# A third pair of convolution projections by seven quarter products instead of two full chunks, with its weight sums in DRAM

## The chip, the cores and the metric

The kernel runs on one core of a Trainium2 chip. The metric is the device time of one execution in microseconds (us), the median of three runs. Besides, one execution was taken with the hardware profiler; its trace gives each engine's instructions, waits and transfers. The engines are PE (matrix products; PEld is its weight load), DVE (vector), ACT (scalar engine), POOL (GpSimd, which here mostly issues transfers) and SP (which issues the weight loads).

## The reference

One block of an encoder in float32, 512 tokens by 1024 features: a short gated convolution and a four-head retention side by side, merged by gates, then a feed-forward part.

```python
h = rmsnorm(x, g_mix)
proj = h @ w_in
xc, gb, gc, q, k, v, g_sw, gate_a, gate_r = split(proj)   # xc, gb, gc: 1024 columns each
u = gc * xc
conv = sum(u_pad[:, tap:tap + s] * w_conv[tap] for tap in range(3))
y_a = (gb * conv) @ w_a_out
ret = group_norm(retention_fwd(q, k, v) + retention_bwd(q, k, v))   # 4 heads
y_r = (ret * silu(g_sw)) @ w_r_out
x = x + (sigmoid(gate_a) * y_a + sigmoid(gate_r) * y_r) @ w_o
h2 = rmsnorm(x, g_ffn)
x = x + (silu(h2 @ w_ff_gate) * (h2 @ w_ff_up)) @ w_ff_down
return rmsnorm(x, g_final)
```

The change is about `xc` and `gc` (called x and C here), about a quarter of their columns: 512 to 767.

## The kernel before

**Products.** Float32 is kept by splitting each operand into a rounded part (hi) and the rest (lo). A product of two such pairs takes three matmuls, hi by hi, hi by lo and lo by hi (`mm3`, lines 337 to 341). For a weight tile (128 x 1024) this means: the raw tile is loaded by SP into the pool `raw` (10 buffers), ACT casts it to hi (line 200), DVE subtracts to get lo (line 201), both in the pool `wpool` (5 pairs).

**Two ways to do a projection.** A *chunk* is 256 columns of `w_in`: two loads of 512 KB, and `feature_major` (line 347) with 2 x 8 x 3 = 48 matmuls of 512 token columns (lines 339 to 341). A *quad* does two chunks at once by a scheme of seven products in place of eight (`fm_quad`, line 383): the weights of both are cut into quarters, sums of quarters are formed (t1 to t4), and each of the forms b11, t1, t2, b21, t3, t4, b22 is multiplied by a form of the activations. Each such product (`prod`, line 372) has 2 x 4 x 3 = 24 matmuls of 256 columns (line 380). The first product is copied out of its PSUM bank by ACT (`snap`, line 429, its copy at line 431) before the third product (t2) is added in the same bank; further copies stand behind t2 and t3.

**Sums of weights.** For most quads the sums t1 to t4 are formed by DVE on the raw tiles (line 298). For the quads listed in `SUMMED` they are formed in DRAM ahead of time: POOL issues a copy (line 271) and an accumulating transfer (line 269) for each sum, one step of the list at a time, behind stores of the v and gate projections (`sum_step`, line 262). Before the change these are the first two quads of the feed-forward part.

**Order of the work.** After a start-up and the q and k of three heads come six quads of v, swish gate and branch gates in a token-major form (line 424, up to 323.6 us), then `mix_quads` (line 821): a quad each for x and C of parts 0 and 1 of the convolution (a part is 256 columns), and one for B of both. Behind each quad of x and C stands the convolution (`conv`), behind the third quad `z_forms` (line 782): ACT and DVE split the results into hi and lo, and POOL stores them to DRAM (`z<-t`, line 626); they are read back for the product with `w_a_out` much later. Then `load_head(0)` loads q (hi, lo: `qh`, `ql`), a table, v and the gate of the first head; `do_scores` forms its scores (24 matmuls), `split_v` splits v, `do_mix(2)` does part 2 of the convolution by three chunks x, C and B, and the loop over the heads begins with `do_pv`; part 3 follows inside the loop by three chunks.

The plan is a list of weight units in the order of use; weights are loaded `LEAD` = 4 units ahead of the one that is prepared and prepared (cast, subtract) `AHEAD` = 2 units ahead of their use. A scheduler places the instructions of all engines in their final order, so that independent work (scores, chunks, quads) may be mixed on PE. Small tiles of 128 x 512 for copies and for hi and lo of the stores come from one pool of 9 buffers (`t512`); a buffer that a store reads is free when the store has landed.

Of the kernel before, what the change touches and what calls it, by code (L numbers as in the profile page):

```python
# [1 line left out]

# [1 line left out]

# [65 lines left out]
    return (q, "b21"), (q + 1, "b11") if q + 1 < NQ else None  # L70


def plan():

    out = []  # L80

    def a(name, col):
        out.append(("c", name, 0, 8, col, 256))

    def b(name, row, nk, col, nc):
        out.append(("c", name, row, nk, col, nc))

    def quad(c0, c1):
        for name in FORMS:
            for u in (0, 2):  # L90
                out.append(("q", ("w", c0, c1), name, u, 2))

    for h in range(EARLY):
        for r in (0, 512):
            b("w_in", r, 4, (C_Q + h * QK, C_K + h * QK), 512)
    for h in range(HEADS):
        quad(C_V + h * VD, C_G + h * VD)
        if h >= EARLY:
            a("w_in", C_Q + h * QK)
            a("w_in", C_K + h * QK)  # L100
    for c in (0, 512):
        quad(C_GA + c, C_GR + c)
    for c0, c1 in ((C_XC, C_GC), (C_XC + 256, C_GC + 256), (C_GB, C_GB + 256)):
        for name in FORMS:
            out.append(("q", ("x", c0, c1), name, 0, 4))
    for s in (2, 3):
        for c in (C_XC, C_GC, C_GB):
            a("w_in", c + s * 256)
    for h in range(HEADS):
        for c in (0, 512):  # L110
            b("w_r_out", h * VD, 4, c, 512)
    for name in FORMS:
        for u in (0, 2):
            out.append(("q", ("a",), name, u, 2))
    for r in (0, 512):
        for c in (0, 512):
            b("w_o", r, 4, c, 512)
    def f(q, *names):
        for n in names:
            out.append(("q", ("f", q), n, 0, 4))  # L120

    for q, name in FIRST_PRODUCTS:
        f(q, name)
    for q0, n in FF_PARTS:
        for q in range(q0, q0 + n):
            between, behind = beside(q)
            f(q, "t1", "t2")
            if between:
                f(*between)
            f(q, "t3")  # L130
            if behind:
                f(*behind)
            f(q, "t4", "b22")
        units = [(name, u) for name in FORMS for u in range(0, n, 2)]
# [13 lines left out]

SUMMED = (("f", 0), ("f", 1))


def loads():
# [17 lines left out]
def block_kernel(ctx: ExitStack, tc: tile.TileContext, xw0, xw, xT, xtok, wpack, wquad, cols, decs, rot, g_ffn, g_final, out):  # L172
# [15 lines left out]
    def bigtile(dt=F32, n=4):  # L188
        return big.tile([P, n, 512], dt, tag="big", name="big", padded_shape=[P, 4, 512])
# [28 lines left out]
    pos = [0]  # L218
    block = [0]

    made = []
    ready = []

# [8 lines left out]
    def prefetch_block(loads, splits, inbig):  # L232
        i = block[0]
        block[0] += 1
        st = [rawtile(), rawtile()]
        units = []
        for c in range(2):
            if loads:
                loads(c)
            nc.sync.dma_start(st[c], wpack[i][:, c * QH:(c + 1) * QH])  # L240
        for c in range(2):
            hi, lo = unit(inbig)
            units.append((hi, lo))
            split(st[c], hi, lo)
            if splits:
                splits(c)
        return units
# [6 lines left out]
    def quarter(quad, name, u=0):  # L254
        return wquad[next(i for i, x in enumerate(QUARTERS) if x[1:4] == (quad, name, u))]

    steps = [(quad, f, g, add) for group in (
        (("t1", "b11", 0), ("t3", "b22", 0)), (("t1", "b12", 1), ("t3", "b12", 1)),
        (("t2", "t1", 0),), (("t2", "b22", 1),), (("t4", "t2", 0),), (("t4", "b21", 1),))
        for quad in SUMMED for f, g, add in group]  # L260

    def sum_step(behind=None):

# [165 lines left out]
    def snap(ps):  # L429
        t = t512()  # L430
        nc.scalar.copy(t, ps)  # L431
        return t
# [305 lines left out]
    def do_quad(left, right, func, func_left=None):  # L738
        def ev_sum(dst, o, f):
            def ev(tt, t):  # L740
                if f:
                    nc.scalar.activation(t, t, f)
                last = store(dst[:, o + tt, :], t)
                if tt and not o:
                    sum_step(last)
            return ev

        def ev21(tt, ps):
            t = t512()
            nc.scalar.activation(t, ps, func_left or AF.Copy)  # L750
            last = store(left[:, 2 + tt, :], t)
            if tt:
                turn_one()
                sum_step(last)
        strassen(4, xforms, ev_sum(left, 0, func_left), ev21, ev_sum(right, 2, func), ev_sum(right, 0, func))
# [12 lines left out]
    def conv(m, b, u, c):  # L768

        nc.scalar.activation(c, u[:, 0:512], AF.Copy, scale=wconv[:, 3 * b:3 * b + 1])  # L770
        for tap in (1, 2):
            nc.vector.scalar_tensor_tensor(
                out=c, in0=u[:, tap:tap + 512], scalar=wconv[:, 3 * b + tap:3 * b + tap + 1],
                in1=c, op0=ALU.mult, op1=ALU.add)

    def u_tile():
        u = misctile(2 * 514, "u").rearrange("p (m n) -> p m n", m=2)
        nc.vector.memset(u[:, :, 0:1], 0.0)
        nc.vector.memset(u[:, :, 513:514], 0.0)
        return u  # L780

    def z_forms(s, z):

        x1, x2 = z[:, :, 0:256], z[:, :, 256:512]

        def put(j, t):
            n = t.shape[1]
            hl = [t512(F32R)[:, 0:256 * n].rearrange("p (f t) -> p f t", f=n) for _ in range(2)]
            split(t, *hl)
            for d, x in zip(zd[j], hl):  # L790
                store(d[:, :, s, :], x.bitcast(F32))
# [9 lines left out]
    def do_mix(s):  # L801
        us, c = [], bigtile()[:, 0:2, :]
        feature_major(xg, lambda m, ps: us.append(snap(ps)))
        u = u_tile()

        def ev_c(m, ps):
            nc.vector.tensor_tensor(out=u[:, m, 1:513], in0=ps, in1=us[m], op=ALU.mult)
            conv(m, 2 * s + m, u[:, m], c[:, m])
        feature_major(xg, ev_c)

        def ev_b(m, ps):
            nc.vector.tensor_tensor(out=c[:, m], in0=ps, in1=c[:, m], op=ALU.mult)
        feature_major(xg, ev_b)
        z_forms(s, c)

    T1, T2 = slice(0, 256), slice(256, 512)

    def halves(t):
        return t.rearrange("p (m t) -> p m t", m=2)

    def mix_quads():

        c = bigtile().rearrange("p (s m) t -> p s m t", s=2)
        for s in range(2):
            u, got = u_tile(), {}

            def ev21(ps):
                nc.vector.tensor_tensor(out=u[:, :, 257:513], in0=halves(ps), in1=halves(got["c2"]), op=ALU.mult)

            def ev12(t):  # L830
                nc.vector.tensor_tensor(out=u[:, :, 1:257], in0=halves(got["x1"]), in1=halves(t), op=ALU.mult)
            fm_quad(xf, lambda t: got.update(x1=t), ev21, lambda t: got.update(c2=t), ev12)
            for m in range(2):
                conv(m, 2 * s + m, u[:, m], c[:, s, m])

        def times(s, t):
            def ev(b):
                o = c[:, s, :, t]
                nc.vector.tensor_tensor(out=o, in0=halves(b), in1=o, op=ALU.mult)
            return ev  # L840
        fm_quad(xf, times(0, T1), times(0, T2), times(1, T2), times(1, T1))
        for s in range(2):
            z_forms(s, c[:, s])


    def load(src, dt=F32):
        t = bigtile(dt)
        nc.sync.dma_start(t if dt == F32 else t.bitcast(F32), src)
        return t

    def load_head(h):
# [76 lines left out]
                    nc.vector.tensor_tensor(out=t, in0=t, in1=sgr[half][:, nb, :], op=ALU.mult)  # L928
            token_major(yr, 0, 1, ev)

    mix_quads()
    nxt = load_head(0)
    p = do_scores(nxt[0], nxt[1])
    vv, sg = split_v(nxt[2]), nxt[3]
    do_mix(2)
# [419 lines left out]
```

## Time and profile before

| what | value |
|---|---|
| time of the runs, median (lowest to highest) | 1027.11 us (1026.5 to 1027.32) |
| the profiled execution | 1027.93 us, its span 1026.1 us |
| granted PE clock | 0.999 |
| PE busy | 1018.1 us of the span |
| LDWEIGHTS (PEld) busy | 887.9 us |
| DVE busy / ACT busy / POOL busy | 886.3 / 535.5 / 125.0 us |
| moved by DMA | 187.66 MB |

A row of a group in the profile has the line, engine, operation, the tiles (out<-in), the shape and the count, then the busy time and the mean of one in ns, then the idle time of the engine ahead of them and what ended it. A row of the timeline or the chain has the start in us and the duration. Matmuls are pipelined, and their ends are modelled: how many follow each other in a stretch tells more than the duration of one. In the order of the program the numbers behind a tile's name tell its buffers apart; a row has a line, an operation and its tiles, and `waits` names semaphores, those of DMAs (DMAHW for SP's, DMASW for POOL's) among them.

### The profile page before, as it was taken

What the parts mean: (1) busy time and instruction counts of PE and PEld (TensorE: products, weight loads), DVE (VectorE), ACT (ScalarE), POOL (GpSimd) and SP (SyncE); (2) the same over time, 40 slices, a digit from 0 to 9 for tenths busy, and PEclk for the clock granted to TensorE, in tenths of its full rate; (3) what the DMA queues carried; (4) which work ended last, traced back from release to release, by engine and by line L of the source; (5) the groups of instructions that cost most, each with busy time, mean ns of one, the idle gap of its engine ahead of it and who ended that gap; (6) DMA issues with size and microseconds to landing.
All of it is one profiled execution on the core that took longest, in us unless ns stands there. A gap on an engine that the chain in (4) does not pass through costs nothing.

```text
span 1026.1 us, 14780 instructions
## 1 busy us (share of the span) xinstructions
PE 1018.1 (99%) x5610; PEld 887.9 (87%) x5610; DVE 886.3 (86%) x1151; ACT 535.5 (52%) x728; POOL 125.0 (12%) x205
## 2 busy tenths in 40 slices
PE   9999999999999999999999999999999999999997
PEld 7888888888888998888888888889998999899986
DVE  7878998969798988797999998569998999889996
ACT  7547655553656455342542334356654565556554
POOL 0030231222212003202011000000002000110011
PEclk9999999999999999999999999999999999999999
DMA  9525597794767657828177525633318522663513
GB/s 346 195 83 183 172 299 211 213 312 153 255 203 238 254 200 256 323 81 314 52 277 285 208 94 176 236 102 121 122 44 220 177 87 83 193 156 103 164 29 96
DMA packets 51304, 187.66 MB, mean 183 GB/s; under 512 B 6880, under 2 KB 7008, under 8 KB 47264
## 3 DMA queue, kind: packets, MB, share of 16 engines
q1 hardware_dynamic: 36448, 133.19, 37.5%
q0 software_dynamic: 14496, 53.23, 17.5%
q8 instruction: 44, 0.72, 0.3%
q10 hardware_dynamic: 288, 0.29, 0.1%
q14 instruction: 28, 0.23, 0.1%
HBM read 148.14 MB, written 46.92 MB: 190 GB/s over the span
## 4 chain that ended last, share of the span: by engine, by line
PE 97%; DVE 1%; DMA 1%; issue 0%; POOL 0%; ACT 0%; POOLq 0%; DVEq 0%; ACTq 0%
PE bank L424 34%; PE bank L380 28%; PE bank L339 11%; PE bank L341 11%; PE bank L340 11%; DMA raw<-wquad 1%; PE bank L470 0%; PE bank L1030 0%; PE bank L981 0%; PE bank L655 0%; DVE wlo L201 0%; DVE raw L298 0%; DVE big L1229 0%; DVE t L445 0%; POOL fin L1219 0%
## 5 line engine op out<-in xcount | busy, mean ns | idle before, releaser
L200 ACT CAST whi<-raw 128x1024 fp32r<-128x1024 f32 (+2 forms) x291 | 294.5, 1028 | 278.7 <-PE bank L424 60.0
L201 DVE TENSOR_TENSOR wlo<-raw,whi 128x1024 fp32r<-128x1024 f32 (+2 forms) x292 | 343.9, 1193 | 81.6 <-ACT whi L200 81.1
L380 PE MATMUL bank<-xform,whi 128*128 128x256 f32 x1424 | 257.6, 284 | 0.2 <-ACT whi L200 0.2
L380 PEld LDWEIGHTS bank<-xform,whi 128*128 128x128 f32 x1424 | 222.4, 192 | 1.2 <-ACT t L431 0.5
L380 PE MATMUL bank<-xform,wlo 128*128 128x256 f32 x712 | 201.5, 283 | 0.0
L424 PE MATMUL bank<-whi,big 128*128 128x512 f32 x596 | 187.6, 390 | 0.0
L298 DVE TENSOR_TENSOR raw<-raw 128x1024 f32<-128x1024 f32 (+1 forms) x128 | 152.1, 1206 | 3.8 <-DMA raw<-wquad 2.8
L380 PEld LDWEIGHTS bank<-xform,wlo 128*128 128x128 f32 x712 | 136.8, 192 | 0.0
L424 PEld LDWEIGHTS bank<-whi,big 128*128 128x128 f32 x596 | 112.0, 188 | 23.8 <-ACT t L431 0.4
L424 PE MATMUL bank<-whi,xform 128*128 128x512 f32 x384 | 121.3, 390 | 0.0
L424 PE MATMUL bank<-wlo,big 128*128 128x512 f32 x298 | 116.2, 390 | 0.0
L431 ACT COPY t<-bank 128x512 f32<-128x512 f32 x105 | 61.0, 585 | 56.3 <-PE bank L380 29.7
L339 PE MATMUL bank<-big,whi 128*128 128x512 f32 x220 | 85.8, 390 | 0.0
L341 PE MATMUL bank<-big,wlo 128*128 128x512 f32 x220 | 85.7, 390 | 0.0
L340 PE MATMUL bank<-big,whi 128*128 128x512 f32 x220 | 85.7, 390 | 0.0
L424 PEld LDWEIGHTS bank<-whi,xform 128*128 128x128 f32 x384 | 72.1, 188 | 15.1 <-DVE xform L201 0.2
L424 PE MATMUL bank<-wlo,xform 128*128 128x512 f32 x192 | 74.8, 390 | 0.0
L339 PE MATMUL bank<-whi,big 128*128 128x512 f32 x176 | 69.0, 392 | 0.0
L340 PE MATMUL bank<-wlo,big 128*128 128x512 f32 x176 | 68.6, 390 | 0.0
L341 PE MATMUL bank<-whi,big 128*128 128x512 f32 x176 | 68.2, 390 | 0.0
L424 PEld LDWEIGHTS bank<-wlo,big 128*128 128x128 f32 x298 | 56.0, 188 | 11.4
L340 PEld LDWEIGHTS bank<-big,whi 128*128 128x128 f32 x220 | 41.3, 188 | 8.6
(205 smaller groups left out, 1394.8 us busy)
## 6 DMA issues: line engine op xcount, KB each, us to landing
raw<-wquad SPq DMA_DIRECT2D x132, 512.0 KB, 4.6
raw<-wpack SPq DMA_DIRECT2D x50, 512.0 KB, 5.3
z<-t POOLq DMA_DIRECT2D x24, 256.0 KB, 4.7
zform<-z POOLq DMA_DIRECT2D x6, 1024.0 KB, 6.0
v<-t POOLq DMA_DIRECT2D x16, 256.0 KB, 5.3
sg<-t POOLq DMA_DIRECT2D x16, 256.0 KB, 5.0
qh<-t POOLq DMA_DIRECT2D x16, 256.0 KB, 3.0
ql<-t POOLq DMA_DIRECT2D x16, 256.0 KB, 3.6
```

Of the source, the lines that this page charges most:

```text
L200: first = (round or nc.scalar.copy)(hi, src)
L201: nc.vector.tensor_tensor(out=lo, in0=src, in1=hi.bitcast(F32), op=ALU.subtract)
L298: nc.vector.tensor_tensor(out=t, in0=t, in1=raws[quad, more, u][:, 0:n], op=ALU.add)
L339: nc.tensor.matmul(ps, lh, rh, start=first, stop=False)
L340: nc.tensor.matmul(ps, lh, rl, start=False, stop=False)
L341: nc.tensor.matmul(ps, ll, rh, start=False, stop=last)
L380: nc.tensor.matmul(o, l[:, c], r[:, k], start=start and s == 0 and k == 0 and i == 0, stop=stop and k == 3 and i == 2, skip_group_check=True)
L424: nc.tensor.matmul(pss[tt], l, r[:, c], start=start and k == 0 and i == 0, stop=stop and k == n - 1 and i == 2, skip_group_check=True)
L431: nc.scalar.copy(t, ps)
```

## The change

Part 2's x and C become a quad: seven products of 256-column matmuls stand in for two chunks.

- The plan gets a fourth quad, `XC`, behind the quad of B, and loses the chunks of x and C of part 2. `do_mix(2)` does the chunk of B alone.
- The code of a quad of x and C moves out of `mix_quads` into `xc_quad(s, c)`, and `mix_quads` ends with `load_head(0)` and `xc_quad(2, ...)`; so the seven products stand ahead of the scores in the program.
- `XC` joins `SUMMED`: its t1 to t4 are formed in DRAM by eight more steps on POOL. These go first, and the steps of the feed-forward part behind them; `sum_step` is now called at one more place of each quad of the early stage (24 calls for 24 steps, in place of 18 for 16).
- The loads of the chunks (`prefetch_block`) that come after are kept behind the last load of the head by `issue_after`.

```diff
+XC = ("x", C_XC + 512, C_GC + 512)
...
-    for c0, c1 in ((C_XC, C_GC), (C_XC + 256, C_GC + 256), (C_GB, C_GB + 256)):
+    for c0, c1 in ((C_XC, C_GC), (C_XC + 256, C_GC + 256), (C_GB, C_GB + 256), XC[1:]):
         for name in FORMS:
             out.append(("q", ("x", c0, c1), name, 0, 4))
     for s in (2, 3):
-        for c in (C_XC, C_GC, C_GB):
+        for c in (C_GB,) if s == 2 else (C_XC, C_GC, C_GB):
             a("w_in", c + s * 256)
...
-SUMMED = (("f", 0), ("f", 1))
+SUMMED = (XC, ("f", 0), ("f", 1))
...
-            nc.sync.dma_start(st[c], wpack[i][:, c * QH:(c + 1) * QH])
+            with tc.issue_after(behind[-1].ins) if behind else nullcontext():
+                nc.sync.dma_start(st[c], wpack[i][:, c * QH:(c + 1) * QH])
...
+    steps = sums_of(SUMMED[:1]) + sums_of(SUMMED[1:])
...
-                if tt and not o:
+                if tt:
                     sum_step(last)
...
+    def xc_quad(s, c):
+        u, got = u_tile(), {}
+        def ev21(ps):
+            nc.vector.tensor_tensor(out=u[:, :, 257:513], in0=halves(ps), in1=halves(got["c2"]), op=ALU.mult)
+        def ev12(t):
+            nc.vector.tensor_tensor(out=u[:, :, 1:257], in0=halves(got["x1"]), in1=halves(t), op=ALU.mult)
+        fm_quad(xf, lambda t: got.update(x1=t), ev21, lambda t: got.update(c2=t), ev12)
+        for m in range(2):
+            conv(m, 2 * s + m, u[:, m], c[:, m])
...
         for s in range(2):
             z_forms(s, c[:, s])
+        head = load_head(0)
+        behind.append(last[-1])
+        part2.append(bigtile()[:, 0:2, :])
+        xc_quad(2, part2[0])
+        return head
...
     def do_mix(s):
-        us, c = [], bigtile()[:, 0:2, :]
-        feature_major(xg, lambda m, ps: us.append(snap(ps)))
...
+        if s == 2:
+            c = part2[0]
+        else:
+            us, c = [], bigtile()[:, 0:2, :]
+            feature_major(xg, lambda m, ps: us.append(snap(ps)))
...
-    mix_quads()
-    nxt = load_head(0)
+    nxt = mix_quads()
     p = do_scores(nxt[0], nxt[1])
```

What the change does to the order is shown at three places.

PE before, at the end of the scores of the first head (banks 3593) and the start of the chunk of x (bank 3623):

```order
L339 MATMUL bank_3593<-big_3550 128x512
L340 MATMUL bank_3593<-big_3552,big_3550 128x512
L341 MATMUL bank_3593<-big_3550,big_3552 128x512
L339 MATMUL bank_3623<-big_419,whi_3429 128x512
L340 MATMUL bank_3623<-big_421,whi_3429 128x512
```

In the order before, the chunk of x follows the scores at once.

PE now, at the same place: the end of the product of t2 of the new quad (bank 3582), the last three score matmuls (bank 3839), four matmuls of the chunk of B (bank 3868), then the product of t3.

```order
L390 MATMUL bank_3582<-xform_686,whi_3587 128x256 x2
L390 MATMUL bank_3582<-xform_686,wlo_3588 128x256
L349 MATMUL bank_3839<-big_3570 128x512
L350 MATMUL bank_3839<-big_3572,big_3570 128x512
L351 MATMUL bank_3839<-big_3570,big_3572 128x512
L349 MATMUL bank_3868<-big_423,whi_3739 128x512
L350 MATMUL bank_3868<-big_425,whi_3739 128x512
L351 MATMUL bank_3868<-big_423,wlo_3740 128x512
L349 MATMUL bank_3868<-big_423,whi_3739 128x512
L390 MATMUL bank_3582<-xform_682,whi_3645 128x256 x2
L390 MATMUL bank_3582<-xform_682,wlo_3646 128x256
```

The chunk of x is gone from behind the scores, and the new quad is spread around them: its products of b11, t1 and b21 stand ahead of 21 of the 24 score matmuls, t2 ahead of the last three, t3 behind four matmuls of the chunk of B, t4 behind seven more, and b22 behind t4.

ACT before, behind the third quad: the last casts of `z_forms` (t512), then casts of the scores (big_3558) and of v (big_3604), then the copy of the first half of x (bank 3623) and weights of a chunk.

```order
L200 CAST t512_3520<-big_2806 128x512 [waits DVE_49]
L200 CAST t512_3530<-t512_3518 128x512 [waits DMASW3_49,DVE_49,Activation_49]
L200 CAST t512_3536<-t512_3519 128x512 [waits DMASW5_49,DVE_49,Activation_49]
L200 CAST t512_3542<-big_2806 128x256 [waits DMASW2_49,DVE_49]
L200 CAST big_3558<-t512_3567 128x512 [waits DVE_49]
L200 CAST big_3558<-t512_3578 128x512 [waits DVE_49]
L200 CAST big_3604<-big_3554 128x1024 [waits DMAHW1_49]
L200 CAST big_3558<-t512_3589 128x512 [waits DVE_49]
L200 CAST big_3604<-big_3554 128x1024
L200 CAST big_3558<-t512_3600 128x512 [waits DVE_49]
L431 COPY t512_3648<-bank_3623 128x512 [waits DMASW4_49,DMASW3_49,PE_49]
L200 CAST whi_3688<-raw_3681 128x1024 [waits DMAHW6_49,PE_49]
```

ACT now, at the same place: the copies of bank 3582, on which the products of t2, t3 and t4 wait, stand behind casts of `z_forms` and of weights (whi_3739, whi_3743 and whi_3860 are the chunk of B's and its successor's).

```order
L204 CAST whi_3704<-raw_3585 128x1024 [waits DMAHW7_49,PE_49]
L204 CAST t512_3540<-big_2818 128x512 [waits DVE_49]
L204 CAST whi_3739<-raw_3735 128x1024 [waits DMAHW0_49,PE_49,Activation_49]
L204 CAST t512_3550<-t512_3538 128x512 [waits DMASW3_49,DVE_49]
L204 CAST t512_3556<-t512_3539 128x512 [waits DMASW5_49,DVE_49,Activation_49]
L204 CAST t512_3562<-big_2818 128x256 [waits DMASW7_49,DMASW1_49]
L441 COPY t512_3615<-bank_3582 128x512 [waits DMASW1_49]
L204 CAST whi_3743<-raw_3736 128x1024 [waits DMAHW1_49,PE_49]
L441 COPY t512_3673<-bank_3582 128x512 [waits DMASW2_49,DVE_49,PE_49]
L204 CAST whi_3860<-raw_3856 128x1024 [waits DMAHW2_49,PE_49]
L441 COPY t512_3732<-bank_3582 128x512 [waits DVE_49,PE_49]
L204 CAST whi_3864<-raw_3857 128x1024 [waits DMAHW3_49,PE_49]
```

The casts of the scores and of v moved behind these rows, and three copies of the new quad came among the casts that were there. The first of these copies waits for a store on POOL (DMASW1). Its buffer, t512_3615, is that of the lo tile t512_3541, which belongs to the cast t512_3540 in the second row: DVE makes it, POOL stores it, and the buffer is free when that store has landed.

SP before, at the loads around the first head: first a chunk, then all five loads of the head.

```order
L240 DMA raw_3425<-wpack 128x1024
L240 DMA raw_3426<-wpack 128x1024
L848 DMA big_3550<-qh0_215 128x2048
L848 DMA big_3552<-ql0_216 128x2048
L853 DMA tab_3548<-tab0_211 128x896
L848 DMA big_3554<-v0_223 128x2048
L848 DMA big_3556<-sg0_227 128x2048
L240 DMA raw_3611<-wpack 128x1024
```

SP now: the loads of the head stand between those of the new quad, and the chunk of B (wpack) behind them.

```order
L293 DMA raw_3345<-t1x512_81 128x1024
L876 DMA big_3570<-qh0_219 128x2048
L293 DMA raw_3378<-t2x512_82 128x1024
L881 DMA tab_3568<-tab0_215 128x896
L293 DMA raw_3411<-wquad 128x1024
L293 DMA raw_3445<-t3x512_83 128x1024
L293 DMA raw_3476<-t4x512_84 128x1024
L876 DMA big_3572<-ql0_220 128x2048
L876 DMA big_3574<-v0_227 128x2048
L876 DMA big_3576<-sg0_231 128x2048
L293 DMA raw_3585<-wquad 128x1024
L247 DMA raw_3735<-wpack 128x1024
```

The rows of q-lo, v and the gate moved behind five loads of the new quad; the last quarter, b22 (raw_3585), moved behind the head.

More of the change, by code (lines that the diff above doesn't have):

```diff
@@ L1 @@
-from contextlib import ExitStack
+from contextlib import ExitStack, nullcontext
 import numpy as np
@@ L219, in block_kernel @@
     block = [0]
+    behind = []
     made = []
@@ L255, in quarter, with sums_of @@
         return wquad[next(i for i, x in enumerate(QUARTERS) if x[1:4] == (quad, name, u))]
[L257 to L260, printed above, removed]
+    def sums_of(quads):
+        return [(quad, f, g, add) for group in (
+            (("t1", "b11", 0), ("t3", "b22", 0)), (("t1", "b12", 1), ("t3", "b12", 1)),
+            (("t2", "t1", 0),), (("t2", "b22", 1),), (("t4", "t2", 0),), (("t4", "b21", 1),))
+            for quad in quads for f, g, add in group]
+    steps = sums_of(SUMMED[:1]) + sums_of(SUMMED[1:])
     def sum_step(behind=None):
@@ L799, in z_forms @@
         put(3, x2[:, 1:2])
-    def do_mix(s):
-        us, c = [], bigtile()[:, 0:2, :]
-        feature_major(xg, lambda m, ps: us.append(snap(ps)))
[L804 to L814, printed above, removed]
     T1, T2 = slice(0, 256), slice(256, 512)
@@ L819, in halves @@
         return t.rearrange("p (m t) -> p m t", m=2)
+    def xc_quad(s, c):
[7 more added lines that the diff above has]
+            conv(m, 2 * s + m, u[:, m], c[:, m])
+    part2 = []
     def mix_quads():
@@ L824, in mix_quads @@
         for s in range(2):
[L825 to L834, printed above, removed]
+            xc_quad(s, c[:, s])
         def times(s, t):
@@ L843, in mix_quads, with do_mix, ev_c, ev_b @@
             z_forms(s, c[:, s])
+        head = load_head(0)
[3 more added lines that the diff above has]
+        return head
+    def do_mix(s):
+        if s == 2:
[3 more added lines that the diff above has]
+            feature_major(xg, lambda m, ps: us.append(snap(ps)))
+            u = u_tile()
+            def ev_c(m, ps):
+                nc.vector.tensor_tensor(out=u[:, m, 1:513], in0=ps, in1=us[m], op=ALU.mult)
+                conv(m, 2 * s + m, u[:, m], c[:, m])
+            feature_major(xg, ev_c)
+        def ev_b(m, ps):
+            nc.vector.tensor_tensor(out=c[:, m], in0=ps, in1=c[:, m], op=ALU.mult)
+        feature_major(xg, ev_b)
+        z_forms(s, c)
+    last = []
     def load(src, dt=F32):
         t = bigtile(dt)
-        nc.sync.dma_start(t if dt == F32 else t.bitcast(F32), src)
+        last.append(nc.sync.dma_start(t if dt == F32 else t.bitcast(F32), src))
         return t
```

## The prediction

> **What bounds the kernel now.** I read the page's shares first, then the chain that ended last, then the waits of PE, and last the stage around the first head's scores, where the change lies.
>
> ```profile
> span 1026.1 us, 14780 instructions
> PE 1018.1 (99%) x5610; PEld 887.9 (87%) x5610; DVE 886.3 (86%) x1151; ACT 535.5 (52%) x728; POOL 125.0 (12%) x205
> PE 97%; DVE 1%; DMA 1%; issue 0%; POOL 0%; ACT 0%; POOLq 0%; DVEq 0%; ACTq 0%
> ```
>
> ```profile
> PE bank L470 <- DVE t L467: 1.4, 1, 1.4
> PE bank L380 <- ACT whi L200: 0.2, 1, 0.2
> ```
>
> PE carries 97% of the chain, and the waits of PE's queue come to 1.6 us in all, 1.4 of them at the start. So PE's stream bounds the kernel, a microsecond less of it is a microsecond of the end, and there are no idle times that an earlier load or a moved sum could win back. A busy PE may hide a stretched pitch, so the price of a matmul is read from the distance of many. Two pieces of the chain give it, one of 512-column matmuls and one of 256-column matmuls:
>
> ```profile
> 602.38 38.08 PE bank L424 x168
> 903.70 71.99 PE bank L380 x600
> ```
>
> 38.08 / 168 = 0.2267 us, and 71.99 / 600 = 0.1200 us. The 256-column matmul costs 0.53 of the other: per column 6% more. Inside the stage the first is confirmed: from one row to the next lie 30 matmuls of a chunk in 6.80 us, 0.2267 each.
>
> ```profile
> 396.17 0.39 PE L339 MATMUL bank<-big,whi 128*128 128x512 f32 x1
> ...
> 402.97 0.39 PE L339 MATMUL bank<-big,whi 128*128 128x512 f32 x1
> ```
>
> The stage, in windows (busy us and count of PE, PEld, DVE, ACT, POOL, then granted clock, DMA share, GB/s):
>
> ```profile
> 374.00:380.00 6.00, 6.00 (x47) 5.75 (x46) 5.22 (x6) 4.86 (x6) 0.00 (x0) 1.00 0.82 275
> 380.00:390.00 10.00, 10.00 (x67) 9.04 (x66) 9.68 (x16) 4.75 (x8) 3.25 (x6) 1.00 0.93 317
> 390.00:400.00 10.00, 10.00 (x45) 8.28 (x45) 7.76 (x17) 3.89 (x7) 7.28 (x12) 1.00 0.95 333
> 400.00:410.00 10.00, 10.00 (x46) 8.27 (x44) 8.56 (x11) 6.34 (x9) 0.00 (x0) 1.00 0.47 145
> 410.00:420.00 10.00, 10.00 (x46) 8.29 (x45) 5.32 (x8) 1.85 (x4) 0.00 (x0) 1.00 0.97 397
> ```
>
> PE is full in each, at the whole clock; DVE is nearly full for ten of these microseconds, and the DMA engines are close to full in three of the five. PE is the bound, but the change adds work in a place where the cover is thin.
>
> **PE's own work.** Two chunks go: 2 x 48 matmuls x 0.2267 = 21.76 us. Seven products come: 7 x 24 = 168 matmuls x 0.1200 = 20.16 us. The sum is -1.60 us. Seven eighths of the columns would be -2.72 us; the narrower matmul gives 1.1 us of that back. All of it lies on the path.
>
> The Trainium skill speaks against the change here ("TensorE: Matmul & The Clock Gate", "Back-to-back issue gap"): it gives about 81 ns a matmul sustained at 128 columns and 131 ns at 512, which as an estimate is 98 ns at 256 columns and would make the swap 168 x 0.098 - 96 x 0.131 = +3.9 us. The pieces above have 120 and 227 ns in this kernel, so the measurement decides.
>
> **DVE and ACT.** A weight tile costs these two (cast and subtract), and a copy or a product of 512 columns these:
>
> ```profile
> L200 ACT CAST whi<-raw 128x1024 fp32r<-128x1024 f32 x8 | 8.4, 1052 | 14.8 <-PE bank L340 9.2 <-issue 3.8 <-PE bank L380 1.8
> L201 DVE TENSOR_TENSOR wlo<-raw,whi 128x1024 fp32r<-128x1024 f32 x10 | 12.1, 1222 | 3.9 <-ACT whi L200 3.9
> L431 ACT COPY t<-bank 128x512 f32<-128x512 f32 x3 | 1.7, 580 | 0.0
> L839 DVE TENSOR_TENSOR big<-t,big 128x512 f32<-128x512 f32 x3 | 2.1, 687 | 0.0
> ```
>
> Seven tiles stand in for four: ACT gets 3 x 1.05 and one more copy (three, where the chunk of x had two), 0.58, so 3.7 us. DVE gets 3 x 1.22 and three more tensor operations, 3 x 0.69, so 5.7 us. In the 46 us above DVE is busy 36.5 and ACT 21.7: with these they are at 42.2 and 25.4 of the 44.4 us that are left, so neither becomes the bound as a whole. That cost I put at nothing, covered by PE; what remains is the order in which they come.
>
> **The product of t2.** Here I expect a new wait. It adds to the bank that the first copy reads, and ACT comes to that copy only behind casts of the third quad's results and of the chunk of B, and its buffer must have been stored. Before, PE passed from products to scores and back here:
>
> ```profile
> 378.77 0.23 PE bank L339
> ```
>
> ```profile
> 380.39 5.95 PE bank L380 x48
> ```
>
> Between the two rows lie the first seven score matmuls; now 13 matmuls of b11 stand there, 13 x 0.12 = 1.56, as long. Then come the last two products of the third quad (48 x 0.12, to 386.2), the rest of b11 (11 x 0.12, to 387.5), t1 and b21 (2.88 each, to 390.4 and 393.3), and 21 score matmuls (4.76, to 398.1). That is when PE wants t2.
>
> ACT and DVE: the buffer of t1's weights is free at 390.4; cast of b22, 1.05, its subtract, 1.22, then the subtract of the stored tile, 0.69: 393.4, or up to 394.0 as DVE is nearly full. POOL issues the store then, and it has to land. Stores of this kind in the profile from 370 to 440 us have this spread (least, median, most), and two waits on such a landing stand there already:
>
> ```profile
> DMA to landing us min/median/max: 2.7/3.9/5.4
> ```
>
> ```profile
> 394.39 0.69 DVE L201 TENSOR_TENSOR t<-t,t 128x512 fp32r<-128x512 f32 x1 [1.18 <-DMA z<-t]
> ```
>
> ```profile
> 391.03 3.35 POOL L626 DMA_DIRECT2D z<-t  x5 [0.23 <-DVE t L201]
> ```
>
> POOL issues five in a row at 0.67 us each, and the landings in the window from 388 to 398 lie at 4.6 us in the median. I take 4.6, since the DMA engines are as full there (0.93 to 0.95): 394.0 + 4.6 = 398.6, the copy 0.58, so t2 may start at 399.2, 1.1 us after PE is ready. The ends are 393.4 + 2.7 + 0.58 = 396.7, no wait, and 394.0 + 5.4 + 0.58 = 400.0, a wait of 1.9. The casts on ACT ahead of the copy are no later: the one of B's weights needs b21's buffer, 393.3 + 1.05 and three casts of at most 0.62 make 396.2.
>
> ```profile
> DMA to landing us min/median/max: 3.1/4.6/5.1
> ```
>
> The Trainium skill has ACT and DVE as strict first-in, first-out ("Perfetto Trace Analysis", "Tensor Engine Instruction"), by which the copy can't pass those casts. No row here shows an overtaking; with it the wait would still hang on the store.
>
> **The products of t3 and t4.** Behind the end of t2 ACT has a cast of B's weights, 1.05, and the copy, 0.58, together 1.63; PE has three score and four chunk matmuls between, 7 x 0.2267 = 1.59. The same stands between t3 and t4. I take 0.1 for both together; the ends are nothing and 0.3 each, if semaphores cost as much as the 0.2 us wait in PE's list. The two b22 and `do_pv` follow with DVE close behind (conv, v and B's product are all DVE's): nothing, up to 0.3 if its extra 5.7 us aren't taken up by the 1.4 and 4.7 us that it is free in the windows from 400 to 420.
>
> **Loads.** Before, the head's loads went out by 352 us for scores at 378.6:
>
> ```profile
> 351.94 0.37 SPq L848 DMA_DIRECT2D big<-sg  x1
> ```
>
> ```profile
> raw<-wquad SPq DMA_DIRECT2D x132, 512.0 KB, 4.6
> ...
> big<-sg SPq DMA_DIRECT2D x4, 1024.0 KB, 11.3
> ```
>
> Now q-lo, v and the gate stand behind five loads of the new quad, and the scores need them at 393.3. If they go out by 355 and take 11.3 us, 27 us are left: nothing. Behind them on SP stand b22 and the chunks: b22's raw tile is wanted at 390.4, its buffer is that of t3's tile of the third quad, which is prepared two products ahead of its use (the 24 matmuls ahead of 378.77, so from 375.9), and it is free at about 372, and 512 KB take 4.6 us: nothing, and if DMA were twice as slow still nothing. The quad reads three tiles of 512 KB more than the chunks, 1.5 MB, some 4 us at the 397 GB/s of the last window; the window with 145 GB/s takes them.
>
> **The sums in DRAM.** Eight transfers on POOL run between stores of the early quads. The nearest rows, the last of them the landing of the additions:
>
> ```profile
> 141.55 0.54 POOL L626 DMA_DIRECT2D sg<-t  x1 [0.91 <-ACT t L742]
> ...
> 148.88 0.56 POOL L626 DMA_DIRECT2D qh<-t  x1 [2.45 <-ACT t L200]
> ...
> 154.99 0.59 ACT L431 COPY t<-bank 128x512 f32<-128x512 f32 x1 [0.73 <-PE bank L424]
> ```
>
> ```profile
> DMA to landing us min/median/max: 5.6/8.6/9.7
> ```
>
> One step holds POOL's queue: t4's copy needs t2's addition, which now goes out behind the store of 141.55, at 142.1, and lands 8.6 us later, at 150.7. The store of 148.9 behind it goes out at some 151.3, and ACT's copy of 155.0 may need its buffer: 3 us of landing make it 154.3. Behind that copy stand casts of weights; they are two units ahead of their use, and a unit keeps PE for 12 x 0.2267 = 2.7 us, so PE has about 4.5 us of cover. I take nothing; with the longest landing, 9.7, ACT is 0.4 us late, and the cover holds it.
>
> **The sum.** -1.60 + 1.1 + 0.1 = -0.4 us. Against the profiled execution (1027.93, span 1026.1, 1.8 us around it) that is 1027.5; it lay 0.8 above the median of the runs, so 1027.11 - 0.4 = 1026.7 us for the median. Three runs here spread 0.8 us; 0.2% (2 us) is about what a measurement of this kernel can tell from no change.
>
> **The rivals.** (a) Everything is covered: the store lands within 3.5 us. Then the whole 1.60 comes, 1025.5 us. For it speaks the least of 2.7 us and that PE waits nowhere in the stage before; against it that DVE already waits for such stores at 394. (b) Slower: the store lands late, since more weight tiles are loaded in this stage than before. With a landing L the wait at t2 is 394.0 + L + 0.58 - 398.1 = L - 3.5; from 5.0 on the gain is gone, and at 8.6, as the additions take in the median, the wait is 5.1 and the kernel at 1027.11 - 1.60 + 5.1 + 0.1 = 1030.7. Against it: no store of this kind took more than 5.4. (c) The sums on POOL make PE wait in the early stage: with a landing L of the addition ACT's copy is L - 9.3 late, and PE L - 13.8; at 17.2, twice the median, that is 3.4 more than forecast, 1030.1. (d) Weight loads bind at 256 columns:
>
> ```profile
> L380 PEld LDWEIGHTS bank<-xform,whi 128*128 128x128 f32 x1424 | 222.4, 192 | 1.2 <-ACT t L431 0.5
> ```
>
> 168 x 0.192 - 21.76 = +10.5 us, 1037.6. The 0.1200 of the long piece, less than 0.192, is against it: weight loads overlap. The estimate by the spacing rule above, +3.9 us or 1031.0, is this rival's milder form. The Trainium skill would judge by weight loads as well: "Perfetto Trace Analysis", "Identifying the Most-Contended Engine", has PE's distance from its limit read from LDWEIGHTS and not from matmul time. (e) The change doesn't do as it says: the products come, but the plan keeps the chunks; the order shows them gone, so no chance.
>
> **Chances.** The forecast, a part given back, 0.58; (a) 0.27; (b) 0.09; (c) 0.05; (d) 0.01. The forecast's ends: the lower one is (a), and -1.60 + 1.9 + 0.6 + 0.3 = +1.2 is the upper, 1028.3; with 0.4 for the scatter of a median they are 1025.1 and 1028.7. The range 1025.1 to 1028.7 leaves out most of (b), (c) and (d), 0.15. Faster by over 0.2% needs below 1025.06, the lower edge of (a): 0.08. Slower needs above 1029.16: (b) and (c) in their upper part and (d), 0.11. The rest, 0.81, is the same.
>
> **What would show it.** In the profile after: PE's products at L390 between 374 and 424 at 0.12 us; one wait of PE at t2, near 398, of about 1 us, ended by ACT's copy at L441, whose own wait is ended by a transfer z<-t; small ones at t3 and t4; DVE fuller in 400 to 420. It would be wrong if the wait isn't there or is over 2 us, if a copy or cast near 155 delays PE, or if 256-column matmuls are wider than 0.12 us.

## The result and the profile after

| | median of the runs | lowest to highest | ratio to before, 95% interval |
|---|---|---|---|
| before (6 runs) | 1027.21 us | 1026.5 to 1027.49 | |
| after (6 runs) | 1033.64 us | 1033.25 to 1034.61 | 1.0065 [1.0055, 1.0076] |

The change makes the kernel 6.4 us slower. The prediction had 1026.7 us, the same within 0.2%, and a range that ended at 1028.7. The profiled executions differ by 5.4 us of span (1026.1 and 1031.5; the one of before is the longest among the runs shown, the one of after the shortest of its own), and the rest of this section accounts for these.

The page of after, its shares and the chain:

```profile
span 1031.5 us, 14954 instructions
...
PE 1019.1 (99%) x5682; PEld 890.8 (86%) x5682; DVE 889.1 (86%) x1157; ACT 538.4 (52%) x732; POOL 128.3 (12%) x213
...
PE 78%; issue 14%; DVE 4%; DMA 2%; POOL 2%; ACT 0%; POOLq 0%; SPq 0%; DVEq 0%; ACTq 0%
```

The chain falls from 97% on PE to 78%: it now leaves PE somewhere. The waits of PE tell where:

```profile
PE bank L390 <- ACT t L441: 4.3, 1, 4.3
PE bank L480 <- DVE t L477: 1.4, 1, 1.4
```

The second is the start of the kernel, as before. The first is new, and it is the wait at the product of t2 that the prediction named. Its place in the timeline: the last score matmul ahead of it, the last cast on ACT ahead of the copy, the copy of the bank, and the first matmuls of t2.

```profile
397.79 0.39 PE L351 MATMUL bank<-big 128*128 128x512 f32 x1
...
398.69 0.40 ACT L204 CAST t<-big 128x256 fp32r<-128x256 f32 x1 [1.73 <-DMA z<-t]
401.84 0.58 ACT L441 COPY t<-bank 128x512 f32<-128x512 f32 x1 [2.75 <-DMA z<-t]
...
402.48 0.50 PE L390 MATMUL bank<-xform,whi 128*128 128x256 f32 x2 [4.30 <-ACT t L441]
```

PE is ready at 397.79 + 0.23 = 398.0 (forecast: 398.1) and starts t2 at 402.48, 4.46 us later (forecast: 1.1). The copy itself was held by a transfer z<-t, the store of the lo tile whose buffer it takes. That store went out on POOL at 394.19 (forecast: 394.0). Its row, and its landing:

```profile
394.19 0.68 POOL L636 DMA_DIRECT2D z<-t  x1 [1.10 <-DVE t L806]
```

```profile
DMA to landing us min/median/max: 7.6/7.6/7.6
```

The time at which PE is ready and the time of the store are as forecast. The landing is not: 7.6 us, 394.2 to 401.8, and not 4.6. The casts ahead of the copy are late as well, at an end of 399.1 in place of 396.2, for the last of them waits for a store too; the copy waits 2.75 us beyond that. The stores between 386 and 402 us, least, median and most, before and after:

```profile
DMA to landing us min/median/max: 2.8/4.1/5.1
```

```profile
DMA to landing us min/median/max: 3.1/6.9/7.8
```

The transfers of the same window show who came between. Before (queue q1 is SP's; its numbers are packets, MB, and the time of its packets as a share of that of the 16 engines):

```profile
q1 hardware_dynamic: 435, 1.57, 31.1%
...
z<-t POOLq DMA_DIRECT2D x10, 256.0 KB, 4.1
raw<-wpack SPq DMA_DIRECT2D x2, 512.0 KB, 5.0
```

After:

```profile
q1 hardware_dynamic: 822, 3.00, 58.3%
...
raw<-wpack SPq DMA_DIRECT2D x5, 512.0 KB, 8.1
z<-t POOLq DMA_DIRECT2D x10, 256.0 KB, 7.2
```

SP moves 3.00 MB here and not 1.57, five weight loads in place of two, and both kinds of transfer land later. The first two go out at the same times as before, 385.73 (385.75 before) and 390.04 (390.07); the three behind them are new. These loads are for chunks far ahead in the plan (the end of part 3 and the product with `w_r_out`). They go out now because SP waits only for a free raw tile, and the new quad frees raw tiles just here. The issues on SP from 390 us on, each shown alone:

```profile
390.04 0.33 SPq L247 DMA_DIRECT2D raw<-wpack  x1
```

```profile
392.11 0.33 SPq L247 DMA_DIRECT2D raw<-wpack  x1
```

```profile
393.21 0.33 SPq L247 DMA_DIRECT2D raw<-wpack  x1
```

```profile
395.95 0.33 SPq L247 DMA_DIRECT2D raw<-wpack  x1
```

And DVE's subtracts that end the use of a raw tile:

```profile
388.76 1.22 DVE L205 TENSOR_TENSOR wlo<-raw,whi 128x1024 fp32r<-128x1024 f32 x1
...
390.83 2.35 DVE L205 TENSOR_TENSOR wlo<-raw,whi 128x1024 fp32r<-128x1024 f32 x2
...
394.71 1.21 DVE L205 TENSOR_TENSOR wlo<-raw,whi 128x1024 fp32r<-128x1024 f32 x1
```

By the plan's order they are those of t3, t4 and b22 and of the first tile of the chunk of B. They end at 389.98, 392.05 and 393.18, and 395.92: every load follows one of them by less than 0.1 us. Before, SP issued nothing between 390.4 and 400.6.

The wait has a second price. The windows behind it (as in the prediction, the third number from the end is the granted clock):

```profile
402.00:403.00 1.00, 0.52 (x4) 0.52 (x5) 0.54 (x1) 0.43 (x1) 0.00 (x0) 1.00 1.02 410
403.00:404.00 1.00, 1.00 (x7) 1.00 (x7) 0.15 (x1) 0.00 (x0) 0.00 (x0) 0.55 0.94 369
404.00:405.00 1.00, 1.00 (x7) 1.00 (x6) 0.00 (x0) 0.00 (x0) 0.00 (x0) 0.50 0.32 123
405.00:406.00 1.00, 1.00 (x6) 1.00 (x6) 0.00 (x0) 0.00 (x0) 0.00 (x0) 0.50 0.07 29
406.00:407.00 1.00, 1.00 (x8) 1.00 (x8) 0.00 (x0) 0.00 (x0) 0.00 (x0) 0.74 0.00 0
```

The clocks of the windows say for how long PE ran at half: 0.9 us of the second, the next two whole, and 0.5 of the last, so 3.4 us, from 403.1 to 406.5. Its matmuls follow each other there by 0.213 us and not by 0.120: sixteen of them lose 1.5 us, with PE busy in every window from 403 on.

The balance of the two spans, from the starts of all matmuls against their pitch: the swap -1.60; the wait +4.46; the clock +1.5; small waits at t2's second matmul, t3 and t4 +0.4; two waits in the scores of a later head, at 514 and 526 us, +0.76; against that a wait of 0.5 near 790 us in before's profile that is not in after's; +0.3 of trifles elsewhere, the start of the kernel among them. That is +5.3, and the spans differ by 5.4.

### The profile page after: what moved, and what is told of

Read it like the earlier page. It is cut to its first block, busy times and chain, and to the rows that moved or that the text cites. A ratio compares the mean times of both kernels' runs of the same rounds, so it can differ in the third digit from the quotient of the medians.

```text
span 1031.5 us, 14954 instructions
## 1 busy us (share of the span) xinstructions
PE 1019.1 (99%) x5682; PEld 890.8 (86%) x5682; DVE 889.1 (86%) x1157; ACT 538.4 (52%) x732; POOL 128.3 (12%) x213
## 4 chain that ended last, share of the span: by engine, by line
PE 78%; issue 14%; DVE 4%; DMA 2%; POOL 2%; ACT 0%; POOLq 0%; SPq 0%; DVEq 0%; ACTq 0%
PE bank L434 34%; PE bank L390 22%; PE bank L349 7%; PE bank L350 7%; PE bank L351 7%; DMA z<-t 1%; DVE big L219 1%; POOL z L636 1%; DMA big<-ql 1%; PE bank L480 0%; DVE big L920 0%; DVE big L205 0%; DVE wlo L205 0%; PE bank L1057 0%; PE bank L1008 0%
## 5 line engine op out<-in xcount | busy, mean ns | idle before, releaser
L204 ACT CAST whi<-raw 128x1024 fp32r<-128x1024 f32 (+2 forms) x294 | 297.6, 1028 | 276.4 <-PE bank L434 61.0
L390 PE MATMUL bank<-xform,whi 128*128 128x256 f32 x1488 | 270.7, 284 | 4.3 <-ACT t L441 4.3
L390 PEld LDWEIGHTS bank<-xform,whi 128*128 128x128 f32 x1488 | 233.2, 193 | 5.8 <-ACT t L441 5.6
L390 PE MATMUL bank<-xform,wlo 128*128 128x256 f32 x744 | 210.9, 284 | 0.0
L390 PEld LDWEIGHTS bank<-xform,wlo 128*128 128x128 f32 x744 | 143.4, 193 | 0.0
L349 PE MATMUL bank<-big,whi 128*128 128x512 f32 x188 | 73.3, 390 | 0.0
L351 PE MATMUL bank<-big,wlo 128*128 128x512 f32 x188 | 73.2, 389 | 0.0
L350 PE MATMUL bank<-big,whi 128*128 128x512 f32 x188 | 73.2, 389 | 0.0
L219 DVE STREAM_TRANSPOSE big<-big 32x512 f32<-32x512 f32 x64 | 45.0, 703 | 1.7 <-ACT big L922 0.9
```

The costliest lines, as they stand in the source:

```text
L204: first = (round or nc.scalar.copy)(hi, src)
L219: nc.vector.transpose(o[:, :, :, b, :], i[:, :, :, q, :])
L349: nc.tensor.matmul(ps, lh, rh, start=first, stop=False)
L350: nc.tensor.matmul(ps, lh, rl, start=False, stop=False)
L351: nc.tensor.matmul(ps, ll, rh, start=False, stop=last)
L390: nc.tensor.matmul(o, l[:, c], r[:, k], start=start and s == 0 and k == 0 and i == 0, stop=stop and k == 3 and i == 2, skip_group_check=True)
```

## The experiments

Each kernel is the changed one with the edit shown. In e1, e3, e5, e7 and e9 the order of PE moves as well: with no wait for the copy in sight, t2 stands ahead of b21 and of the scores, and the scores come later. In e4 the orders of PE, ACT and DVE change a little, but t2 stays behind the scores. In e2, e6 and e8 PE, ACT and DVE have the changed kernel's order, and only loads move. The waits and landings are those of one profiled execution of each kernel.

| | median (runs) | before beside it | ratio, 95% interval | wait of PE at the quad | landing of the 256 KB stores, 386 to 402 us |
|---|---|---|---|---|---|
| after | 1033.64 (6) | 1027.21 | 1.0065 [1.0055, 1.0076] | 4.46 | 7.2 |
| e1 own buffers for two copies | 1028.03 (10) | 1027.09 | 1.0015 [1.0004, 1.0025] | 2.3, third copy | 7.7 |
| e2 four loads held | 1027.68 (10) | 1027.09 | 1.0004 [0.9995, 1.0013] | 0.8 | 4.1 |
| e3 stores behind the quad | 1027.94 (10) | 1027.09 | 1.0007 [0.9997, 1.0016] | none; 0.5 at 421.8 | (one store) |
| e4 sums by DVE | 1028.28 (10) | 1027.09 | 1.0011 [1.0002, 1.0020] | 0.8; 0.4 at 422.9 | 4.3 |
| e5 own two, four held | 1026.38 (11) | 1027.27 | 0.9990 [0.9981, 0.9999] | none | 3.1 |
| e6 two held | 1031.58 (5) | 1027.27 | 1.0036 [1.0024, 1.0048] | 2.1 | 5.0 |
| e7 own three | 1026.18 (10) | 1027.27 | 0.9993 [0.9984, 1.0002] | none | 7.3 |
| e8 one held | 1033.05 (4) | 1026.98 | 1.0054 [1.0039, 1.0069] | 4.6 | 7.1 |
| e9 own three, four held | 1025.82 (11) | 1026.98 | 0.9989 [0.9980, 0.9997] | none | 3.2 |

**e1, the copies in buffers that no store reads.** Part 2's tile has four planes, of which two are used; `copy` lets ACT copy into the next of the tiles given, and takes a small buffer as before when none is left.

```diff
-        p1 = snap(a)
+        p1 = copy(a)
...
-        part2.append(bigtile()[:, 0:2, :])
-        xc_quad(2, part2[0])
+        both = bigtile()
+        part2.append(both[:, 0:2, :])
+        xc_quad(2, part2[0], [both[:, 2, :], both[:, 3, :]])
```

> The changed kernel, but the first two copies of the new quad go into the free half of part 2's big tile, so that they need no buffer that a store reads. Theory S (the copy waits for the landing of a store of the third quad's results, and PE's clock falls after that idle time): in the profile after, t2 started at 402.48 where PE was ready at 398.01, 4.46 us, and some 1.5 us went to matmuls at 213 ns behind it; both go, and the small waits at t3 and t4 (0.3 us) too. The kernel comes to 1025.6 to 1027.5 us. Rival C (the stage is too full: DMA, DVE and weight loads of the 256-column matmuls slow it wherever the copy stands): PE waits elsewhere instead, and the time stays above 1030.

The median is 1028.03 us, 5.6 below the changed kernel, a little above the range of theory S. The wait at t2 and the slow clock are gone; what is left is the third copy, which still takes a small buffer and stands ahead of t4:

```profile
PE bank L390 <- ACT t L447: 2.2, 1, 2.2
```

```profile
400.94 0.59 ACT L447 COPY t<-bank 128x512 f32<-128x512 f32 x1 [2.17 <-DMA z<-t]
```

The same wait on the same kind of store, one copy later. Rival C asked for a time above 1030 and falls as a cause of the 6.4 us. The runs of this kernel spread from 1026.87 to 1031.64, as they would if the landing differed from run to run; only one execution was profiled, so this isn't shown.

**e2, the loads out of the stores' way.** `HELD` numbers the loads of chunks, and 21 to 24 are the four from 390 us on; `zlast` holds the stores of parts 0 and 1.

```diff
+HELD = range(21, 25)
...
+            late = 2 * i + c in HELD
+            with tc.issue_after((zlast if late else behind)[-1].ins) if behind else nullcontext():
+                (nc.gpsimd if late else nc.sync).dma_start(st[c], wpack[i][:, c * QH:(c + 1) * QH])
```

> The changed kernel, but the four weight loads that went out at 390 to 396 us, beside the stores, go out from POOL behind the last of those stores; the copy still waits for its store. Theory L (those loads share the DMA engines with the stores and took their landing from 4.1 to 7.2 us in the median): landings fall to about 4.5, the wait at t2 to about 1.3 us, and the time to 1028 to 1030 us. Rival Q (the stores are late by POOL's queue or by their number): landings stay at 7, the wait at 4.5, the time at 1033 to 1034.

The copy still waits for its store, on the same engine in the same order, yet the time falls by 6 us:

```profile
z<-t POOLq DMA_DIRECT2D x10, 256.0 KB, 4.1
raw<-wpack POOLq DMA_DIRECT2D x4, 512.0 KB, 6.2
```

```profile
PE bank L393 <- ACT t L444: 0.7, 1, 0.7
```

The landing is back at the 4.1 us of before, and the wait and the time came out a little below what theory L had put. POOL issued the same stores in the same order, so rival Q falls: the loads made the stores late. By the gain of 1.60, this wait and 0.3 of small ones as in the changed kernel, the median would be near 1026.6 us; the other 1 us stays open.

**e3, the stores behind the quad.**

```diff
-        for s in range(2):
-            z_forms(s, c[:, s])
         head = load_head(0)
...
         xc_quad(2, part2[0])
+        for s in range(2):
+            z_forms(s, c[:, s])
```

> The changed kernel, but the results of parts 0 and 1 are split and stored (z_forms) behind the new quad and not ahead of it: the copies wait for no store, with the buffers as they are. Theory S: no wait at t2 and 1025.6 to 1027.5 us, if the casts of the scores, which now stand behind the stored tiles on ACT, are in time for the product with v; if those wait for a store as the copy did, 2 to 4 us come back there. Rival C: above 1030.

1027.94 us, above the range of theory S without a wait, and far below rival C. No copy waits. A part comes back where it was expected, ahead of the product with v, though only 0.5 us of it, so that more than 1 us of this median stays open too:

```profile
PE bank L390 <- ACT whi L204: 0.9, 1, 0.9
PE bank L350 <- DVE big L205: 0.4, 1, 0.4
```

The second row is that wait, at 421.8 us. The first is at 790 us, in the feed-forward part, where the profiles of all these kernels have between 0 and 1.1 us.

**e4, the sums by DVE.**

```diff
-SUMMED = (XC, ("f", 0), ("f", 1))
+SUMMED = (("f", 0), ("f", 1))
...
-                if tt:
+                if tt and not o:
                     sum_step(last)
```

> The changed kernel, but the sums t1 to t4 of the new quad are formed by DVE on raw tiles, as in the other quads, and POOL sums in DRAM only those of the feed-forward part, as before the change. DVE gets 4 more operations of 1.2 us in the stage. Theory S: the first copy still waits for a store (order), so the wait at t2 stays at 3 to 6 us and the time at 1033 to 1037 us. Rival P (the sums in DRAM cost the time, by POOL's queue early or by traffic): the time falls below 1030.

1028.28 us: the number that I had given to rival P, but not by its cause. In the changed kernel the early stage, where POOL makes the sums, costs PE nothing; its six quads are one piece of the chain, as before the change (152.47 us for it there):

```profile
73.30 152.35 PE bank L434 x672
```

What the sums by DVE change is the raw tiles: with four quarters reused in place of seven tiles that come free one by one, no load goes out in the first part of the stores.

```profile
395.60 9.44 SPq L247 DMA_DIRECT2D raw<-wpack  x6
```

```profile
z<-t POOLq DMA_DIRECT2D x10, 256.0 KB, 4.3
```

SP's first load of this window is at 395.6 and not at 390.0, the landing is 4.3 us, and PE waits 0.8 at t2. That wait is no longer one for a store: ACT comes to the copy straight from a cast of weights, which waited for a sum on DVE (the rows before and at the copy).

```profile
397.73 1.05 ACT L204 CAST whi<-raw 128x1024 fp32r<-128x1024 f32 x1 [0.82 <-DVE raw L308]
398.69 0.58 ACT L441 COPY t<-bank 128x512 f32<-128x512 f32 x1
```

My expectation, that the wait would stay, took the order for the cause and left out the landing. The sums in DRAM cost time through the raw tiles that they set free, not through their own traffic: e2 keeps these sums and is as fast.

**e5, both halves of the cause.** The edits of e1 and e2 together.

> Both edits in one: the first two copies of the new quad in the free half of part 2's tile, and the four weight loads held behind the stores. With the copies alone the last copy still waited for a store, 2.3 us of PE; with the loads alone t2 waited 0.8 us. Theory (store wait and loads are the two halves of one cause, and the swap itself gains 1.60 us): both waits go, and the kernel is 1.0 to 1.6 us faster than before, 1025.5 to 1026.1. Rival (256-column products in this stage cost more than their pitch, so nothing is left to gain): 1027 to 1028, with no PE wait that explains it.

1026.38 us, a little above what I had put, and faster than before by 0.9 us; the ratio 0.9990 [0.9981, 0.9999] holds the -1.60 us. In the stage no wait above 0.11 us is left.

**e6 and e8, the dose.** `HELD` is `range(21, 23)` in e6 and `range(21, 22)` in e8.

> A dose: the changed kernel with two of the four loads held behind the stores in place of four; the copies have their old buffers. Theory L: the landing of the stores and the wait at t2 lie between those with none held (7.2 us, 4.46 us) and with four held (4.1 us, 0.82 us), at some 5.7 and 2.6 us, and the time between 1027.7 and 1033.6, near 1029.5, for the lost clock goes with a short wait. If only the first load matters, as with four; if only the last ones, as with none.

> The dose once more: one of the four loads held behind the stores. By theory L the landing and the wait at t2 lie between those with two held (5.0 us, 2.1 us) and with none (7.2 us, 4.46 us): some 3 us of wait and 1030.5 to 1033 us. It also shows the clock of the matmuls behind an idle time of 3 us: after 2.1 to 2.3 us of idle time they kept the full clock in the profiles so far, after 4.5 us sixteen of them ran at half.

With none, one, two and four loads held the landings are 7.2, 7.1, 5.0 and 4.1 us, the waits 4.46, 4.64, 2.12 and 0.82 us, and the medians 1033.64, 1033.05, 1031.58 and 1027.68 us. The rows of e8 and of e6:

```profile
z<-t POOLq DMA_DIRECT2D x10, 256.0 KB, 7.1
raw<-wpack SPq DMA_DIRECT2D x3, 512.0 KB, 8.2
```

```profile
z<-t POOLq DMA_DIRECT2D x10, 256.0 KB, 5.0
raw<-wpack SPq DMA_DIRECT2D x3, 512.0 KB, 5.6
```

Both show three loads on SP: in e8, where all is 0.45 us earlier, a fourth went out at 385.28, just ahead of the window; in e6 one of the three is the load at 385.79. The waits follow the landings, but not the count of loads evenly: the first load held gives nothing (I had expected 3 us of wait and got 4.64), the second gives most. The first is the one that goes out at 390.07 before the change as well; the three that are left in e8, at 391.67, 392.76 and 395.51, are the new ones. e6's median is 2 us above what I had put; its profiled execution, with 2.12 us of wait, is the shortest of its runs (1029.83), and of the three runs at 1031.6 two have a granted clock of 0.996, as the changed kernel's had (0.995 to 0.997). What the wait was in those runs no profile shows.

**e7 and e9, all three copies.** One more big tile takes the third copy; e9 holds the four loads besides.

```diff
+        xc_quad(2, part2[0], [both[:, 2, :], both[:, 3, :], bigtile()[:, 0, :]])
```

> The changed kernel with all three copies of the new quad in tiles of their own (the third in one more big tile), the loads as in the changed kernel, so that the stores land as late as there. Theory S: no PE wait at t2, t3 or t4 though the landings stay above 6 us, and 1025.5 to 1026.8 us; the one more big tile may make a load of the next head later, which I put at 0 to 1 us. If the full DMA engines slow more than the copies, it stays at 1028.

> All three copies in tiles of their own and the four loads held. With three own tiles the loads as they were gave 1.1 us of the 1.60 us in the median, without a wait of PE in the stage. If late landings cost nothing more once the copies don't need them (theory S), this is no better: 1025.6 to 1026.4 us. If full DMA engines still cost something elsewhere, it is 0.5 us or more below that.

e7 is the sharpest of them: the stores land as late as in the changed kernel, and nobody on PE's path waits for them.

```profile
z<-t POOLq DMA_DIRECT2D x10, 256.0 KB, 7.3
```

```profile
PE bank L486 <- DVE t L483: 1.4, 1, 1.4
```

That is all of PE's waits: the start of the kernel. The median is 1026.18 us, 1.1 below before, though the interval just holds no change. The edit moves the order of PE too, so e7 alone doesn't part the buffers from the order; e2, with the order as it was, shows what the landing alone does. e9, 1025.82 us, is faster than before by 0.1%, 0.9989 [0.9980, 0.9997]; that it is better than e7 can't be told from these intervals.

## Why the prediction was wrong

**The swap of matmuls**: right. The gain of 1.60 us was on the path. With all waits taken away e9 gains 1.16 us of it in the median, and its interval, 0.3 to 2.1 us, holds the 1.60. The pitch stayed 0.120 us at the full clock, and weight loads never bound; the estimate of +3.9 us by the Trainium skill ("TensorE: Matmul & The Clock Gate", "Back-to-back issue gap") stays refuted in this kernel.

**The place and the mechanism of the new wait**: right. It is at t2, by ACT's copy, by the landing of the store whose buffer the copy takes; PE was ready 0.1 us from the forecast and the store went out 0.2 us from it.

**The landing**: this is the step that failed. The prediction took "4.6, since the DMA engines are as full there (0.93 to 0.95)", from the window of before, and settled the extra loads with "the window with 145 GB/s takes them". They did not go to the window that had room. SP issues a load as soon as a raw tile is free, and three of the quad's seven tiles and the first of the chunk of B come free between 390 and 396 us, beside the stores. e2 shows it: with the four loads out of the way the landing is 4.1 us and 6 us of the time come back. The share of 0.93 to 0.95 hid the difference: it can't rise much, but the share of SP's queue in it rose from 31.1% to 58.3%, at the stores' cost. The Trainium skill says as much ("DMA: Bandwidth & Descriptors", "Issuing engines are not separate DMA queues"): transfers of SP and POOL run on the same 16 engines and interleave. The traces here agree, with 4.1 against 7.2 us.

**Rival (b)** is what came: its formula, wait = L - 3.5, gives 4.1 us for the landing of 7.6, and 4.46 was measured. It had a chance of 0.09, because no store of before took more than 5.4 us: a maximum of the old traffic, used as a bound for the new.

**The clock** was in no case of the prediction. The wait of 4.46 us made PE slow for 3.4 us behind it, +1.5 us. With the formula and this price rival (b) would have come to 1027.11 - 1.60 + 4.1 + 0.1 + 1.5 = 1031.2. The median is 2.4 us above that: some 1.3 are the longer wait and the small terms of the balance, and 1.1 the place of the two profiled executions among their runs, 0.7 above the median of before and 0.4 below that of after.

**t3 and t4**: forecast 0.1 for both, measured about 0.3. **DVE and ACT, the loads of the head, the sums on POOL**: as forecast, nothing; PE passes the early stage and the start of the scores as before. **`do_pv`**: nothing. The 0.76 us in the scores of a later head were not forecast; other kernels of the study have between 0 and 0.5 there, and their cause wasn't looked into.

## What to carry to other kernels

When a change adds tiles to a pool that throttles a load queue, ask when each tile comes free: the queue will issue a load at that moment, whatever else is in flight, and loads that nobody needs yet can delay a store that somebody waits for. A buffer shared between something on the path (a copy that frees a PSUM bank) and something that is released by a transfer makes the path as late as that transfer; two free planes of another tile took 5.6 us off here, and a third tile the wait that was left. Bounds for a landing must come from the traffic that the change makes, not from the traffic that it finds.

## What the runs showed of the hardware

PE's clock falls behind an idle time of a certain length. After 4.46 us (the changed kernel) and 4.64 us (e8) without a matmul it ran at half for some 3.4 us, with the pitch of the 256-column matmuls at 0.213 us; after 2.12 us (e6), 2.32 us (e1) and 0.82 us (e2) it kept the full clock in the profiles. No run has an idle time between 2.32 and 4.46 us, so the length itself isn't shown. In e8 the fall began about when PE resumed, in the windows from 401 to 403 us (PE idle since 397.6):

```profile
401.00:402.00 1.00, 0.00 (x0) 0.00 (x0) 0.00 (x0) 0.43 (x1) 0.77 (x2) 0.94 1.00 402
402.00:403.00 1.00, 0.79 (x3) 0.79 (x4) 0.69 (x1) 0.15 (x1) 0.33 (x1) 0.50 0.74 287
```

In the changed kernel it came 0.6 us after PE had resumed, so that the first matmuls of t2 still ran at the full clock. The Trainium skill ("TensorE: Matmul & The Clock Gate", "What's actually happening") has this rule: one idle window of about 3.4 us halves the clock, and one busy window of the same length restores it. The traces agree: 4.5 us idle fell, 2.3 us did not, and the slow stretch was 3.4 us long.
